# A table load and idle products ahead of the first transfers, and cross attention's probabilities scaled on VectorE

## The chip, the cores and the metric

The kernel runs on one core of a Trainium2 chip. The metric is device time in microseconds (us) of one execution; the median of the runs is compared. The engines are named as in the profile: PE is TensorE (PEld its weight loads), DVE is VectorE, ACT is ScalarE, POOL is GpSimd, SP is SyncE. A name with a q (ACTq, SPq) is the engine's queue of transfers.

## The reference

All data is float32, 256 tokens of width 1024. The first block mixes grouped attention and a gated spatial unit, adds cross attention over 256 memory tokens, and ends in a mixture of 16 experts. The second block (adaptive scaling, stick-breaking attention, retention, two more mixtures of experts) follows. What the change touches is the entry and this part:

```python
def memory_cross_attention(h, mem_n, w_cq, w_ckv, w_co):
    q = (h @ w_cq).reshape(B, S, X_HEADS, X_HEAD_DIM)          # 4 heads of 128
    kv = mem_n @ w_ckv
    ...
    s = jnp.einsum('bshd,bmhd->bhsm', q, k) * (X_HEAD_DIM ** -0.5)
    p = jax.nn.softmax(s, axis=-1)
    o = jnp.einsum('bhsm,bmhd->bshd', p, v).reshape(B, S, X_WIDTH)
    return o @ w_co
```

## The kernel before

Weights are streamed by SP in units of 1 MB (`Stream.load`, line 125) into a ring of buffers, in a plan written out ahead; a unit is asked for as soon as a buffer is free. A dense product in float32 is made of three products of rounded parts: every unit is split by ACT into a high part (`hl`, line 172, a cast) and by DVE into the rest (line 173), and the activations likewise (`h`, lines 510 and 511). PE then takes, for each quarter of a unit, high by high (line 424), high by rest (425) and rest by high (426). The expert stages use the weights as they are (line 1078).

A scheduler orders each engine's queue from the traced program by its own cost estimates; an instruction given to `keep_in_program_order` stays behind what was traced before it on its engine. The first splits and the `h` tiles are pinned in that way.

`setup` starts the transfers: `xT` on SP, the vectors `vec` on ACT's queue (line 460), the constants `cst`, `cs` and `tri` on POOL's. `block1` begins with the eight `h` tiles, scaled by columns of `vec`, among which the first unit is split in quarters. The first dense product (keys and values, 48 products of 256 columns) is emptied by `ev_kv`, and ahead of that `factors` (line 523) asks for the table that holds both logarithm and exponential (`lnexp`, line 273) and makes the root-mean-square factors of `x` from statistics on DVE (line 313). The next units' casts stand behind this on ACT.

In cross attention `xscores` makes the scores `xs` of a head on PE (line 726), and `softmax` takes the maximum on DVE (line 477), two exponentials with their sums on ACT (line 482), the reciprocal on DVE (line 484) and two scalings on ACT (line 487), each of 128x256. The four heads are traced one behind the other, with pieces of the values' product `cv` between. Then come, for every head, four transposes on PE (`cT`, line 496), a copy to SBUF on ACT (`cTT`, line 498), four products with the values (`co`, line 742), a cast (line 743) and a subtraction (line 744); and then the output's dense product, from line 424 again. `softmax` is also used by the first attention, with eight heads.

`warm(n)` (line 385) issues n products of 128x512 on a column of ones for nothing; the kernel before calls it in the routers and after attention. `lnexp` is an explicit load of a table; other table loads are placed by the compiler ahead of the first function that isn't in the table then loaded.

Of the kernel before, what the change touches and what calls it, by code (L numbers as in the profile page):

```python
# [25 lines left out]
AF = mybir.ActivationFunctionType  # L26
ALU = mybir.AluOpType
# [20 lines left out]
LOOK = [6, 14, 12, 5, 10, 12, 5, 12, 10, 15, 13, 16]  # L48


WARM_LOGITS, WARM_PLACES, WARM_INPUTS, WARM_AFTER = (4, 4, 4), (0, 4, 4), (4, 4, 4), (12, 12)


# [158 lines left out]
class Kernel:  # L212
# [238 lines left out]
    def setup(self):  # L451
        nc = self.nc
        self.C = self.keep("cst", [P, NCST])
        self.V = self.keep("vec", [P, NVEC])
        self.x = self.b8("x")
        self.tri = self.keep("tri", [P, P + 1], F32R)
        nc.gpsimd.memset(self.tri[:, P:].bitcast(F32), 1.0)
        self.ones = self.tri[:, P:]
        self.xT = self.b8("xT", F32, (P, 8, 256))
        nc.scalar.dma_start(self.V[:], self.ap["vec"])  # L460
        for k in (0, 4):
            nc.sync.dma_start(self.xT[:, k : k + 4].rearrange("p k t -> p (k t)"), self.ap["xT"][:, 256 * k : 256 * k + 1024])
        self.cs = self.b2("cs", F32, (P, 2, 2, 32))
        nc.gpsimd.dma_start(self.C[:], self.ap["cst"])
        nc.gpsimd.dma_start(self.cs[:].rearrange("p a t d -> p (a t d)"), self.ap["cs"])
        self.ident = self.cst(C_ID, P)
        tri = self.b2("tri", F32, (P, P))
        nc.gpsimd.dma_start(tri[:], self.ap["tri"])
        nc.gpsimd.tensor_copy(self.tri[:, :P], tri[:])


    def softmax(self, ps, scale, name):

        nc = self.nc
        s3 = ps[:].rearrange("p (a b) -> p a b", a=2)
        m = self.sm(name + "m", [P, 2])
        nc.vector.tensor_reduce(m[:], s3, AX, ALU.max)
        nc.vector.tensor_scalar(m[:], m[:], -scale, None, ALU.mult)
        e = self.b2(name + "e")
        s = self.sm(name + "s", [P, 2])  # L480
        for i in range(2):
            nc.scalar.activation(e[:, i * 256 : (i + 1) * 256], ps[:, i * 256 : (i + 1) * 256], AF.Exp, bias=m[:, i : i + 1], scale=scale, accum_out=s[:, i : i + 1])
        r = self.sm(name + "r", [P, 2])
        nc.vector.reciprocal(r[:], s[:])
        for i in range(2):
            q = e[:, i * 256 : (i + 1) * 256]
            nc.scalar.activation(q, q, AF.Copy, scale=r[:, i : i + 1])
        return e

    def probT(self, e, name):  # L490
# [11 lines left out]
    def block1(self):  # L502
        nc, tc = self.nc, self.tc
# [95 lines left out]
        for c2 in range(0, 5, 2):  # L599
            ps = self.aux("qT")  # L600
# [122 lines left out]
        def xscores(h):  # L723
            s = self.aux("xs")
            for qt in range(2):
                nc.tensor.matmul(s[:, qt * 256 : (qt + 1) * 256], cq[:, h, qt * P : (qt + 1) * P], ck[:, h, :], start=True, stop=True)
            return self.softmax(s, float(128 ** -0.5), "c")

        self.router(0)
        self.offsets(0)  # L730
        es = [xscores(h) for h in range(2)]
        for h in range(2, 4):
            next(fill)
            es.append(xscores(h))
# [1337 lines left out]
```

## Time and profile before

| | |
|---|---|
| runs, median (lowest to highest) | 1316.6 us (1316.1 to 1319.44), 3 runs |
| profiled execution, its own time | 1314.43 us |
| its span, first to last instruction | 1312.8 us |
| PE busy | 1241.5 us, 95% |
| DVE busy | 712.9 us, 54% |
| ACT busy | 405.0 us, 31% |
| POOL busy | 128.0 us, 10% |
| mean granted clock of TensorE | 0.984 |
| moved by DMA | 445.63 MB, mean 339 GB/s |

The profiled execution lies 2.2 us below the median of the runs. Busy shares are means over stages with different limits: PE's products are pipelined and their ends modelled, so 95% does not say that PE works at its peak.

### The profile page before, as it was taken

Reading aid. Unit: us, or ns where it says so; the run is one execution under the profiler, and the core shown is the slowest. Engines: PE = TensorE matmul, PEld = TensorE weight load, DVE = VectorE, ACT = ScalarE, POOL = GpSimd, SP = SyncE. Lnnn points to the kernel's source line nnn. Section 1 sums busy time; section 2 is a strip of 40 time slices with the busy share of each in tenths; the row PEclk is TensorE's granted clock in tenths of the full one; section 3 lists DMA queues with packets and bytes.
Section 4 is the critical chain, followed back from the end, with each engine's and each line's share of the span. In section 5 each row is a group of like instructions: output and inputs, shape, how many; then the busy total and the mean of one; then the engine's idle time right before and its main releaser. Section 6 shows DMA issues by size and latency. Waiting matters only on the chain. (4 is left out here: it accounts for less than half of the span.)

```text
span 1312.8 us, 18783 instructions
## 1 busy us (share of the span) xinstructions
PE 1241.5 (95%) x7149; PEld 784.2 (60%) x7149; DVE 712.9 (54%) x1422; ACT 405.0 (31%) x687; POOL 128.0 (10%) x136
## 2 busy tenths in 40 slices
PE   6999988899999989999999999989999999998995
PEld 5777867754334459977544334488988774433442
DVE  5898996433221149775742222378999754322224
ACT  5675534320100134653310001244345531100011
POOL 1000200000000020332001000130102100000101
PEclk9999998899999999999999999999999999999998
DMA  9857795769999998688499999997788577999992
GB/s 367 344 209 272 270 375 207 306 277 422 420 421 420 420 420 347 233 313 308 190 397 421 420 420 421 419 381 269 269 318 316 199 321 288 413 420 420 420 420 87
DMA packets 64497, 445.63 MB, mean 339 GB/s; under 512 B 7380, under 2 KB 7892, under 8 KB 12048
## 3 DMA queue, kind: packets, MB, share of 16 engines
q1 hardware_dynamic: 62352, 439.91, 83.9%
q10 hardware_dynamic: 1440, 3.13, 0.6%
q8 instruction: 59, 0.97, 0.3%
q0 software_dynamic: 608, 1.32, 0.3%
q14 instruction: 38, 0.31, 0.1%
HBM read 443.28 MB, written 1.05 MB: 338 GB/s over the span
## 5 line engine op out<-in xcount | busy, mean ns | idle before, releaser
L172 ACT CAST hl<-w 128x1024 fp32r<-128x1024 f32 (+1 forms) x160 | 164.7, 1039 | 174.2 <-PE dn L426 105.3
L173 DVE TENSOR_TENSOR hl<-w,hl 128x1024 fp32r<-128x1024 f32 (+1 forms) x154 | 191.4, 1252 | 49.5 <-ACT hl L172 49.3
L1078 PE MATMUL pg<-w,XT 128*64 128x512 f32 (+1 forms) x864 | 174.5, 601 | 0.0
L1078 PE MATMUL pu<-w,XT 128*64 128x512 f32 (+1 forms) x864 | 163.9, 597 | 0.0
L1078 PE MATMUL py<-w,hid 128*64 128x512 f32 (+2 forms) x912 | 155.7, 573 | 2.0 <-ACT hid L1093 2.0
L812 DVE SCALAR_TENSOR_TENSOR acc<-w,sc,acc 128x512 f32<-128x512 f32 x168 | 130.2, 779 | 1.6
L1090 DVE TENSOR_TENSOR hid<-hid,pu 128x512 f32<-128x512 f32 x21 | 14.4, 686 | 203.7 <-PE pu L1078 192.2
L1078 PEld LDWEIGHTS pu<-w,XT 128*64 128x64 f32 (+1 forms) x864 | 50.4, 126 | 96.8 <-issue 95.7
L1078 PEld LDWEIGHTS pg<-w,XT 128*64 128x64 f32 (+1 forms) x864 | 48.0, 125 | 93.2 <-issue 92.1
L1078 PEld LDWEIGHTS py<-w,hid 128*64 128x64 f32 (+1 forms) x912 | 48.8, 125 | 90.7 <-issue 81.8
L1131 DVE TENSOR_TENSOR x<-x,pc 128x512 f32<-128x512 f32 (+1 forms) x90 | 55.0, 647 | 32.8 <-PE pc L1129 32.2
L1066 PE MATMUL px<-O,xs 128*128 128x128 f32 x576 | 70.8, 276 | 0.0
L1399 ACT ACTIVATE hid<-pg 128x512 f32<-128x512 f32 x21 | 12.5, 597 | 187.2 <-PE pg L1078 187.2
L1066 PEld LDWEIGHTS px<-O,xs 128*128 128x128 f32 x576 | 67.2, 192 | 3.4 <-issue 3.4
L1117 DVE SCALAR_TENSOR_TENSOR y<-py,ws,gate 128x512 f32<-128x512 f32 x26 | 19.5, 751 | 66.0 <-PE py L1078 66.0
L1118 ACT CAST yh<-y 128x512 fp32r<-128x512 f32 x26 | 16.1, 618 | 120.8 <-DVE y L1117 120.8
L1070 POOL TENSOR_TENSOR XT<-XT,adaT 128x512 f32<-128x512 f32 x24 | 25.0, 1040 | 289.5 <-DVE XT L1068 289.5
L424 PE MATMUL dn<-hl,h 128*128 128x512 f32 (+1 forms) x128 | 49.4, 391 | 3.4 <-ACT hl L172 3.4
L424 PE MATMUL dn<-hl,e 128*128 128x512 f32 x128 | 51.2, 400 | 0.0
L425 PE MATMUL dn<-hl,h 128*128 128x512 f32 (+1 forms) x128 | 49.7, 388 | 0.8 <-DVE hl L173 0.8
L426 PE MATMUL dn<-hl,e 128*128 128x512 f32 x128 | 49.9, 390 | 0.0
L425 PE MATMUL dn<-hl,e 128*128 128x512 f32 x128 | 49.8, 389 | 0.0
(547 smaller groups left out, 2262.1 us busy)
## 6 DMA issues: line engine op xcount, KB each, us to landing
w<-e SPq DMA_DIRECT2D x282, 1024.0 KB, 14.2
w<-w SPq DMA_DIRECT2D x78, 1024.0 KB, 7.9
w<-wa SPq DMA_DIRECT2D x48, 1024.0 KB, 7.1
w<-e SPq DMA_DIRECT2D x12, 512.0 KB, 16.8
xT<-xT SPq DMA_DIRECT2D x2, 512.0 KB, 5.1
w<-w SPq DMA_DIRECT2D x4, 256.0 KB, 7.5
x<-x SPq DMA_DIRECT2D x2, 512.0 KB, 11.9
mem<-mem SPq DMA_DIRECT2D x2, 512.0 KB, 4.2
```

The lines of the kernel that those rows point to most:

```text
L172: a = k.nc.scalar.copy(hi, w)
L173: b = eng.tensor_sub(lo, w, hi.bitcast(F32))
L424: nc.tensor.matmul(o, a, wh[:, c, :], start=(first and c == 0), stop=False)
L425: nc.tensor.matmul(o, a, wl[:, c, :], start=False, stop=False)
L426: nc.tensor.matmul(o, b, wh[:, c, :], start=False, stop=(last and c == m - 1))
L812: pin(nc.vector.scalar_tensor_tensor(acc[:], w[:, j, :], c, acc[:], ALU.mult, ALU.add))
L1066: nc.tensor.matmul(ps[:, c * P : (c + 1) * P], xs[:, t * D + (k0 + c) * P : t * D + (k0 + c + 1) * P], O[:, t * P : (t + 1) * P].bitcast(F ...
L1070: nc.gpsimd.tensor_add(xo, xo, sh_v[:, k0 : k0 + 4].unsqueeze(2).to_broadcast([P, 4, P]))
L1078: nc.tensor.matmul(out[a : a + w, :], lhs[:, a : a + w], ws[e][(slice(None), c, *h)], start=start, stop=stop, tile_position=(0, a))
L1117: nc.vector.scalar_tensor_tensor(y, py, w, gate[:, n * 512 : n * 512 + 512], ALU.mult, ALU.mult)
L1118: nc.scalar.copy(yh, y)
L1131: nc.vector.tensor_add(a, a, pc)
```

## The change

`setup` asks for the table of logarithm and exponential and issues 20 idle products on the column of ones before its transfers. `softmax` gets a switch by which the two scalings run on DVE, and cross attention sets it; the first attention does not.

```diff
+WARM_START = 20
 WARM_LOGITS, WARM_PLACES, WARM_INPUTS, WARM_AFTER = (4, 4, 4), (0, 4, 4), (4, 4, 4), (12, 12)
...
         nc.gpsimd.memset(self.tri[:, P:].bitcast(F32), 1.0)
         self.ones = self.tri[:, P:]
+        self.lnexp()
+        self.warm(WARM_START)
         self.xT = self.b8("xT", F32, (P, 8, 256))
         nc.scalar.dma_start(self.V[:], self.ap["vec"])
...
-    def softmax(self, ps, scale, name):
+    def softmax(self, ps, scale, name, on_dve=False):
...
         for i in range(2):
             q = e[:, i * 256 : (i + 1) * 256]
-            nc.scalar.activation(q, q, AF.Copy, scale=r[:, i : i + 1])
+            if on_dve:
+                nc.vector.tensor_scalar(q, q, r[:, i : i + 1], None, ALU.mult)
+            else:
+                nc.scalar.activation(q, q, AF.Copy, scale=r[:, i : i + 1])
         return e
...
-            return self.softmax(s, float(128 ** -0.5), "c")
+            return self.softmax(s, float(128 ** -0.5), "c", True)
```

## Rows read from the trace of the kernel before

**Rows 1.** Windows: busy us of each engine, granted clock, DMA share, GB/s.

```profile
260.00:268.00 8.00, 8.00 (x61) 6.78 (x60) 7.05 (x50) 5.61 (x12) 0.00 (x0) 1.00 0.01 3
...
300.00:340.00 40.00, 40.00 (x256) 17.17 (x256) 7.19 (x17) 3.90 (x7) 0.00 (x0) 1.00 1.01 421
```

**Rows 2.** Timeline, 0 to 20 us: start, length, engine, line; idle before.

```profile
0.93 0.41 ACTq L460 DMA_DIRECT2D vec<-vec  x1
...
5.62 1.28 ACT L510 ACT_TABLE_LOAD   x1 [5.62 <-DMA xT<-xT]
...
6.91 0.91 ACT L510 ACTIVATE h<-xT,vec 128x256 fp32r<-128x256 f32 x2
...
9.35 0.62 ACT L172 CAST hl<-w 128x512 fp32r<-128x512 f32 x1 [1.53 <-DMA w<-w]
...
10.02 0.79 PE L424 MATMUL dn<-hl,h 128*128 128x256 f32 x2 [1.59 <-ACT hl L172]
...
14.49 2.00 ACT L172 CAST hl<-w 128x1024 fp32r<-128x1024 f32 x2 [0.57 <-DMA w<-w]
```

**Rows 3.** Windows of the first dense product.

```profile
10.00:14.00 4.00, 3.98 (x17) 3.75 (x18) 4.00 (x9) 3.92 (x9) 1.01 (x2) 1.00 1.02 422
14.00:18.00 4.00, 4.00 (x34) 4.00 (x34) 3.30 (x5) 3.29 (x3) 0.00 (x0) 1.00 1.04 410
```

**Rows 4.** Windows of two stretches ahead of and in cross attention.

```profile
196.00:200.00 4.00, 4.00 (x10) 3.10 (x10) 1.05 (x2) 0.00 (x0) 0.00 (x0) 0.50 0.03 12
...
232.00:236.00 4.00, 2.64 (x11) 2.04 (x11) 0.17 (x1) 2.80 (x9) 0.00 (x0) 0.57 1.01 424
```

**Rows 5.** Timeline of cross attention, 227 to 241 us.

```profile
227.19 1.02 PE L726 MATMUL xs<-ckv,cq 128*128 128x256 f32 x4
...
227.87 0.48 ACT L482 ACTIVATE ce<-xs,cm 128x256 f32<-128x256 f32 x1
...
229.01 0.67 DVE L477 TENSOR_REDUCE cm<-xs 128x2 f32<-128x512 f32 x1
229.13 0.91 ACT L487 ACTIVATE ce<-ce,cr 128x256 f32<-128x256 f32 x2 [0.23 <-DVE cr L484]
...
229.94 0.46 ACT L482 ACTIVATE ce<-xs,cm 128x256 f32<-128x256 f32 x1
...
232.94 0.58 ACT L498 COPY cTT<-cT 128x512 f32<-128x512 f32 x1
...
233.40 0.92 ACT L487 ACTIVATE ce<-ce,cr 128x256 f32<-128x256 f32 x2
...
234.25 1.06 PE L742 MATMUL co<-cTT,ckv 128*128 128x256 f32 x2
...
235.74 4.99 PE L742 MATMUL co<-cTT,ckv 128*128 128x256 f32 x14
...
240.38 0.58 PE L424 MATMUL dn<-hl,o 128*128 128x512 f32 x1
```

**Rows 6.** DMA issues: queue, count, KB each, median us to landing.

```profile
vec<-vec ACTq DMA_DIRECT2D x1, 115.5 KB, 4.8
...
tri<-tri POOLq DMA_DIRECT2D x1, 64.0 KB, 6.4
```

**Rows 7.** Timeline of ACT, 17 to 60 us.

```profile
20.98 0.20 ACT L283 ACTIVATE xn<-xnq 128x2 f32<-128x2 f32 x1 [3.19 <-DVE xnq L321]
...
23.02 3.88 ACT L172 CAST hl<-w 128x1024 fp32r<-128x1024 f32 x4
```

**Rows 8.** Timeline of PE, 20 to 32 us.

```profile
24.12 0.73 PE L424 MATMUL dn<-hl,h 128*128 128x512 f32 x2 [0.67 <-ACT hl L172]
26.01 0.50 PE L424 MATMUL dn<-hl,h 128*128 128x512 f32 x1 [1.15 <-ACT hl L172]
```

**Rows 9.** Groups of DVE by form: count, busy us, mean ns.

```profile
L1663 DVE TENSOR_SCALAR ang<-ang,cst 128x256 f32<-128x256 f32 x1 | 0.3, 350 | 0.0
```

**Rows 10.** Timeline of PE ahead of cross attention's scores.

```profile
195.96 0.79 PE L425 MATMUL cv<-hl,g 128*128 128x512 f32 x1 [3.61 <-DVE hl L173]
```

## The prediction

> **What bounds the kernel now.** I read the page's slices, then the stages by windows, then the two edited places in order of time. Between 300 and 340 us PE is busy for 40 of 40 us while the DMA engines are also full; just before that stage, at 260 to 268, DMA stands at 0.01 with PE full [rows 1]. The expert stages are thus fed by buffers that were filled long before, and they start when the serial work ahead of them is done: a microsecond gained or lost before 260 us moves everything behind it, one for one. Both edits lie before 260 us. So each is worth what it does to the end of its own stage, and I price those two stages alone.
>
> In the first stage the reader is to see who makes PE start at 10.02: the cast of the first weights, which itself waited 1.53 us for their transfer [rows 2]. The granted clock is written as 1.00 from the beginning, but the counts say otherwise: 17 products of 256 columns in 4 us, then 34 of them in the next 4 us, PE busy throughout [rows 3]. The first four microseconds therefore ran at 1.2 GHz and the next at 2.4.
>
> In cross attention ACT is the long queue and PE waits in short pieces. From 232 to 236 us the granted clock is 0.57 [rows 4], and the products of line 742 begin there: 14 of them take 4.99 us [rows 5].
>
> **The change, part by part. The table load.** It leaves 5.62, where it ran 1.28 us as soon as xT had landed, and goes to the head of ACT's queue [rows 2]. The `h` pair behind it can start up to 1.28 us sooner; but the next cast on ACT's queue waits for weights until 9.35 whatever is before it, after 1.53 us of idling [rows 2]. That idling only grows. Worth: 0.
>
> It now stands ahead of the `vec` transfer on the same queue, which went out at 0.93 [rows 2]. Bounds: not delayed at all, or issued at 0.93 + 1.28 = 2.21. Landing took 4.8 us for `vec` itself, 6.4 for the slowest small transfer [rows 6], so `vec` lands at 5.7 at best, 7.0 to 8.6 if delayed. The `h` pair takes 0.91 [rows 2], so it is done by 7.9 to 9.5, against the cast's 9.35. At worst 0.15 us late, and 0.57 us of waiting for the second unit's transfer at 14.49 stands behind as further cover [rows 2]. I take 0.
>
> The trace shows one length for the load, and the work behind it starts 0.01 us after it. The Trainium skill, ScalarE: Activation LUTs, section What ACT_TABLE_LOAD costs, counts a drain as well and arrives at about 2.66 us for a switch. By that figure, as an estimate, `vec` would be issued near 3.6 and land between 8.4 and 10.0, the pair would be done by 10.9, and after the cover some 1.0 us would be lost.
>
> The same table is still asked for by the later call in `factors`, as before; ACT idles 3.19 us just after it, waiting for DVE's statistics [rows 7]. Worth: 0.
>
> **The products for nothing.** They need only the memset, so they run from a little after 1 us. At 1.2 GHz 512 columns take 0.43 us, so 20 of them last 8.5 us at the very most and end by 9.7, before the first real product at 10.02 [rows 2]. With the clock rising after some 4 us, as it did there [rows 3], nine are slow and eleven take 0.235 each: they end near 7.7. Price on PE's path: 0.
>
> What they buy: 17 products at 4.0 / 34 = 0.118 us instead of 4.0 / 17 = 0.235 [rows 3], which is 2.0 us at most; less where a split is not ready. PE was through with all it had at 24.12 - 0.67 = 23.45 [rows 8], and would now be through at 21.45 or later. But the next product needs the cast that ACT starts at 23.02 [rows 7], and PE waited for that cast already, to 24.12, and for another of the same run to 26.01 [rows 8]. ACT got there late because of DVE's statistics of x (the 3.19 us), not because of PE. So the 2.0 us become idle time ahead of 24.12. I take 0; bounds: a gain of 2.0 if ACT's run came earlier too, and a loss (second rival).
>
> **The scaling.** Eight ACTIVATEs of line 487 leave ACT, in four pairs; a pair took 0.91 to 0.92 us [rows 5]. DVE gets eight tensor_scalars of 128x256. The nearest in the trace is the single one of line 1663, of this size, in SBUF, with one factor read from a tile: 350 ns [rows 9]. Consecutive ones overlap a little on this engine: I take 0.62 for a pair, between 0.70 (no overlap) and 0.55.
>
> The direct saving is on the last head alone: 0.92 - 0.62 = 0.3 us.
>
> Against it stands DVE's queue. There the maximum of head 2 (line 477, 0.67 us) begins at 229.01, after head 1's reciprocal [rows 5]. If head 1's pair of scalings goes in between, it begins about 0.55 later, and with it head 2's exponential. In before that exponential began at 229.94, at the instant ACT was through with head 1's scaling (229.13 + 0.91 = 230.04, of which 0.1 overlaps) [rows 5], so there is no slack to absorb it. The same again from head 2 to head 3: +1.1 us. The last head's scaled probabilities, complete at 233.40 + 0.92 = 234.32 in before [rows 5], come at 234.32 + 1.1 - 0.3 = 235.1.
>
> What pays for it is ACT. The copy of head 0's transposed probabilities waited for its turn on ACT until 232.94, and so head 0's product on PE until 234.25; from there 16 products of line 742 and the rest of the transposes stand in a row until 240.38, when line 424 starts [rows 5]. That tail is 240.38 - 234.32 = 6.1 us after the last scaling. With 3.7 us of scaling off ACT, two of the four copies (0.58 each) fit between the exponentials, and two heads' products move into PE's gaps. Eight products of 4.99 / 14 = 0.36 leave the tail: 2.9 us. Sum: 6.1 - 2.9 = 3.2 us of tail after 235.1 gives 238.3, a gain of 2.1. I take 2.0. Bounds: no product moves, 235.1 + 6.1 = 241.2, a loss of 0.8; three heads' products move, 4.3 us off the tail, a gain of 3.5.
>
> **Sum.** 0 + 0 - 2.0 on the profiled execution's own 1314.4 gives 1312.4. That execution stands 2.2 below the median of the runs, 1316.6, so the median should come to 1314.6.
>
> **Rivals.** First, DVE takes the maxima of heads 2 and 3 before the scalings, as they are ready: the last scores are done at 227.19 + 1.02 = 228.2 [rows 5]. Then the exponentials follow each other on ACT without the scalings, 229.94 - 227.87 - 0.91 = 1.16 us a head or less [rows 5], head 3's scaled probabilities are there near 227.87 + 3 x 1.16 + 0.8 = 232.1 instead of 234.3, and the tail is shortened as well or not: a gain of 2.2 to 5, I take 4: 1312.6. Against it: in before these maxima were put after the reciprocal although ready.
>
> Second, PE starves at the start. It would be idle from 21.45 to 24.12, and again up to 26.01, with 0.73 us of work in 4 us [rows 8]. Where PE was starved for 3.61 us at 195.96 [rows 10], the clock read 0.50 in the next 4 us [rows 4]. The Trainium skill (TensorE: Matmul & The Clock Gate, section Why this matters for your kernels) warns in the same sense against idle gaps between bursts; the row agrees. If the clock is lost here, 4 us at half speed after 26.01, the length of the slow start [rows 3], do 2 us of work: +2.0, which leaves 1314.6 + 2.0 = 1316.6.
>
> Third, and slower: DVE's queue delays heads 2 and 3, PE's order stays as it was (+0.8), and the longer gaps bring the low clock sooner or hold it longer, into the first 4 us of line 424: +2 more. 1316.6 + 2.8 = 1319.4. It decides as soon as head 0's product still stands behind head 3's transposes on PE.
>
> Fourth, nothing moves in PE's order and the clock behaves as before: +0.8, 1317.4. Fifth, that the products don't do what they say: if PE's idling from about 7.5 to 10.0 undoes the clock again, the start is as before, and the sum too. Sixth, `vec` lands later than any small transfer here, say at 9.5: the pair is done at 10.4, 1.05 late, 0.57 of it covered: +0.5, 1315.1.
>
> **How the numbers follow.** Forecast (with the fifth, and 0.05 for the sixth, which its own range takes in) 0.45, at 1314.6, itself 1313 to 1316; first rival 0.22; second 0.1; third 0.11; fourth 0.12. The range leaves out the farther part of the first and of the third: 1311.0 to 1319.2. A measurement of this kernel can tell about 0.3%, 3.9 us, from no change: below 1312.7 lie half of the first rival and a share of the forecast in which three heads' products move (0.2 in all); above 1320.5 only a third rival that is worse than priced (0.08); the rest, 0.72, is within.
>
> **What would show it.** Right: PE's early products spaced 0.12 at 11 us, line 424 still waiting for ACT near 24.1; in cross attention a product of line 742 ahead of head 3's transposes, and line 424 near 238. Wrong: `vec` landing after 8.6; a clock of 0.5 after 26; the maxima of line 477 beginning more than 0.6 us after the reciprocal, or before it; or an order of the queues far from the edits that has changed, since a scheduler sets it from its own estimates, and I have priced none of that.

## The result and the profile after

The changed kernel takes 1325.16 us (median of 7 runs, 1316.85 to 1327.24), the kernel before 1316.6 (7 runs, 1314.27 to 1319.44): a ratio of 1.0058, with an interval of 1.0043 to 1.0073. Ratios, here and below, are estimated from all the runs and are not quotients of the medians. The change costs 0.6% where a small gain was forecast, and the time lies above the range. Two later executions at a mean granted clock of 0.94 instead of 0.98, 1333.83 us of the kernel before and 1335.73 of the one with narrow products, belong to a slower state of the chip, and no reading rests on them.

The profiled execution is the quickest of the seven, at 1316.85 us; the other six took 1323.44 or more. So its profile shows what the edits did at their own places, and not where the usual loss is; for that the repeated run below is used. In both kernels the instructions stand in the same order on every engine, apart from the edited ones and one neighbour of theirs on DVE (line 818). Lines have new numbers: 172 is now 173, 424 is 425, 477 to 487 are 480 to 493 (the scaling on DVE is 491), 498 is 504, 742 is 748, 1078 is 1084, 1212 is 1218 and 1368 is 1374.

The start, in the timelines of ACT and of PE (start, length, engine, line; in brackets the idle time and what ended it):

```profile
0.93 1.28 ACT L274 ACT_TABLE_LOAD   x1 [0.93 <-PEq L2070]
0.96 0.40 ACTq L463 DMA_DIRECT2D vec<-vec  x1
5.74 0.91 ACT L516 ACTIVATE h<-xT,vec 128x256 fp32r<-128x256 f32 x2 [3.52 <-DMA vec<-vec]
9.23 0.62 ACT L173 CAST hl<-w 128x512 fp32r<-128x512 f32 x1 [2.59 <-DMA w<-w]
```

```profile
1.09 7.32 PE L386 MATMUL warm<-tri 128*128 128x512 f32 x20 [1.09 <-POOL tri L458]
...
9.90 0.51 PE L425 MATMUL dn<-hl,h 128*128 128x256 f32 x2 [1.28 <-ACT hl L173]
...
23.71 0.73 PE L425 MATMUL dn<-hl,h 128*128 128x512 f32 x2 [1.77 <-ACT hl L173]
25.60 0.51 PE L425 MATMUL dn<-hl,h 128*128 128x512 f32 x1 [1.16 <-ACT hl L173]
```

The load no longer stands between xT and the `h` pair, and `vec` went out at 0.96 while it ran. The idle time ahead of the cast grew from 1.53 to 2.59 us [rows 2]. The 20 idle products end at 1.09 + 7.32 = 8.41, and PE is idle for 1.28 us ahead of the first dense product. Against [rows 8] PE waits 1.77 us for the same cast instead of 0.67, so it was through at 21.94 instead of 23.45, and only 0.41 of these 1.5 us are left at 23.71.

The windows of the first dense product, of cross attention, and of the stretch where the usual loss will be seen:

```profile
10.00:14.00 4.00, 3.78 (x29) 3.56 (x30) 4.00 (x9) 3.96 (x10) 1.27 (x3) 1.00 1.02 421
...
232.00:236.00 4.00, 2.95 (x11) 2.29 (x12) 1.00 (x5) 1.98 (x6) 0.00 (x0) 0.50 1.01 426
236.00:240.00 4.00, 4.00 (x14) 3.31 (x13) 0.85 (x2) 2.18 (x5) 0.00 (x0) 0.66 1.00 416
```

29 products in the first four microseconds instead of 17 [rows 3]: in this execution the early clock was bought. It isn't in every one. The same window of the start alone, one of the experiments below:

```profile
10.00:14.00 4.00, 3.78 (x20) 3.69 (x20) 4.00 (x10) 3.48 (x8) 0.57 (x2) 0.60 1.01 418
```

Cross attention, in the timeline:

```profile
226.69 1.03 PE L732 MATMUL xs<-ckv,cq 128*128 128x256 f32 x4
...
227.37 0.48 ACT L485 ACTIVATE ce<-xs,cm 128x256 f32<-128x256 f32 x1
...
228.43 0.17 DVE L487 RECIPROCAL cr<-cs 128x2 f32<-128x2 f32 x1 [0.50 <-ACT ce L485]
228.51 0.67 DVE L480 TENSOR_REDUCE cm<-xs 128x2 f32<-128x512 f32 x1
229.09 0.60 DVE L491 TENSOR_SCALAR ce<-ce,cr 128x256 f32<-128x256 f32 x2
...
229.62 0.16 DVE L481 TENSOR_SCALAR cm<-cm 128x2 f32<-128x2 f32 x1
229.81 0.47 ACT L485 ACTIVATE ce<-xs,cm 128x256 f32<-128x256 f32 x1 [1.42 <-DVE cm L481]
...
233.22 1.07 ACT L504 COPY cTT<-cT 128x512 f32<-128x512 f32 x2
...
233.63 0.62 DVE L491 TENSOR_SCALAR ce<-ce,cr 128x256 f32<-128x256 f32 x2
...
234.37 1.06 PE L748 MATMUL co<-cTT,ckv 128*128 128x256 f32 x2
...
235.87 4.60 PE L748 MATMUL co<-cTT,ckv 128*128 128x256 f32 x14
...
240.11 0.58 PE L425 MATMUL dn<-hl,o 128*128 128x512 f32 x1
```

DVE takes a third order, which the prediction had not considered: reciprocal of head 1, maximum of head 2, the scalings of head 1, and only then the small multiplication (line 481) for which head 2's exponential waits. ACT idles 1.42 us there, and makes its copies in one piece after the last exponential. The fourth head's scores begin 0.50 us earlier than in [rows 5] and the dense product 0.27 earlier: this stage became 0.2 us longer. The 14 products in a row took 4.60 us here instead of 4.99, so at the same pace it would have been 0.6.

### The profile page after: what moved, and what is told of

It reads as the page before. It is cut to its first block, busy times and chain, and to the rows that moved or that the text cites. A ratio compares the mean times of both kernels' runs of the same rounds, so it can differ in the third digit from the quotient of the medians.

```text
span 1315.3 us, 18828 instructions
## 1 busy us (share of the span) xinstructions
PE 1248.4 (95%) x7169; PEld 789.7 (60%) x7169; DVE 715.1 (54%) x1430; ACT 401.8 (31%) x679; POOL 127.4 (10%) x136
```

## The experiments

Theories: the loss is at the start (PE's waits after the warm start bring the low clock early), in cross attention, or far from both. The kernels differ in their idle products, the place of the load and the scaling's engine.

**The change again.** No edit.

> The changed kernel itself, to see in a trace where its usual execution is longer. Theory A (the granted clock): the queues of both kernels hold the same instructions in the same order but for the edited ones, so no wait has been added; the extra time is stretches at the low clock in the expert stages, behind 250 us, and the trace shows more such windows than the kernel before, with about 8 us in sum. Theory B (a wait): the loss stands in one place, in cross attention or just behind it, with the clock as before. Time by both: 1323 to 1327.

Measured: 1325.11 us (1322.3 to 1326.71) against 1316.17, ratio 1.0064 (1.0051 to 1.0077). Its profiled execution took 1326.69 us and does hold the loss. Its PE timeline in the last expert stage:

```profile
1215.89 0.73 PE L1134 MATMUL pc<-yh,O 128*128 128x512 f32 x2 [1.07 <-ACTq L1374]
1216.62 0.72 PE L1135 MATMUL pc<-yl,O 128*128 128x512 f32 x2
1222.79 1.00 PE L1218 MATMUL pw<-cbr,O 128*128 128x32 f32 x4 [5.45 <-PEq L1374]
```

The same three lines before:

```profile
1210.93 0.73 PE L1128 MATMUL pc<-yh,O 128*128 128x512 f32 x2 [1.06 <-ACTq L1368]
1211.65 0.74 PE L1129 MATMUL pc<-yl,O 128*128 128x512 f32 x2
1212.94 0.62 PE L1212 MATMUL pw<-cbr,O 128*128 128x32 f32 x4 [0.55 <-DVE x L1131]
```

Between two neighbouring products PE waits 5.45 us instead of 0.55, for its own sequencer, at line 1374. That is the branch `with tc.If(more > 0)` which each expert stage has behind its rounds, for extra rounds. All instances of it on PE's sequencer (count; shortest, median and longest in ns; first and last start), in the repeated run, in the profiled execution of after, and before:

```profile
L1374 PEldq COMPARE_BRANCH  x3: 355/388/6004, 393.7 to 1216.6; - x3
```

```profile
L1374 PEldq COMPARE_BRANCH  x3: 358/468/473, 390.6 to 1211.4; - x3
```

```profile
L1368 PEldq COMPARE_BRANCH  x3: 358/367/482, 390.9 to 1211.7; - x3
```

In the repeated run the last of the three branches takes 6.0 us where the others take under 0.5. The profiled execution of after, the quick one, has no such branch.

The repeated run is also 2.8 us late by the end of cross attention. Its windows there and behind the branch:

```profile
24.00:28.00 4.00, 2.84 (x8) 1.96 (x9) 4.00 (x9) 2.77 (x3) 0.00 (x0) 0.80 1.01 422
28.00:32.00 4.00, 4.00 (x15) 3.19 (x15) 1.33 (x2) 0.00 (x0) 0.00 (x0) 0.78 1.01 422
...
1216.00:1222.00 6.00, 1.34 (x4) 0.48 (x4) 1.84 (x3) 0.00 (x0) 1.02 (x2) 0.63 1.02 416
1222.00:1228.00 6.00, 5.21 (x16) 2.21 (x18) 0.63 (x4) 0.00 (x0) 1.85 (x2) 0.51 1.01 416
```

So there are two candidates: the low clock after 26 us, which the second rival foresaw, and the branch with the low clock behind it. Neither theory fits alone: there is a wait, in the last expert stage and not in cross attention, and there are stretches at the low clock.

**The parts alone.** The start alone, the scaling alone, the idle products alone:

```diff
 # the start alone
-            return self.softmax(s, float(128 ** -0.5), "c", True)
+            return self.softmax(s, float(128 ** -0.5), "c")
 # the scaling alone
-        self.lnexp()
-        self.warm(WARM_START)
+        self.warm(0)
 # the idle products alone: no early lnexp(), and the scaling on ACT
-        self.lnexp()
         self.warm(WARM_START)
```

> The load and the 20 idle products at the start, the scaling on ACT as before. If the start costs the time: 1322 to 1327. If the scaling costs it: 1315.5 to 1317, some 0.4 us below the kernel before, which is what the first 60 us gained.

> The scaling on DVE alone, the start as before. If the scaling costs the time: 1322 to 1327. If the start does: 1316 to 1317.5, since line 425 behind cross attention starts within 0.3 us of where it did. If any shift of a fraction of a microsecond costs clock (theory A in its general form), this one and the start alone both come out off the kernel before, by several us.

> The 20 idle products alone, the table load where it was, the scaling on ACT. If the idle products cost the time, by what they do to the clock: 1322 to 1327. If the load or the scaling does: 1316 to 1317.

Measured against 1316.17: the start alone 1323.1, ratio 1.0048 (1.0034 to 1.0063); the scaling alone 1316.45, 1.0009 (0.9997 to 1.002); the products alone 1324.01, 1.0053 (1.0039 to 1.0067). The scaling changes nothing that the median or the ratio can tell, and the products by themselves carry the loss. With them the long branch is there: 6.22 us in the start alone, 6.24 in the products alone, 0.48 at most in the scaling alone.

**Narrow products.** Whether the loss comes from what the products do to PE's clock or from their being in the program: 20 of 16 columns instead of 512.

```diff
-    def warm(self, n):
+    def warm(self, n, cols=512):
...
-        self.lnexp()
-        self.warm(WARM_START)
+        self.warm(WARM_START, 16)
...
-            return self.softmax(s, float(128 ** -0.5), "c", True)
+            return self.softmax(s, float(128 ** -0.5), "c")
```

> 20 idle products of 16 columns instead of 512 ahead of the first transfers, load and scaling as in the kernel before: PE's program is longer by just as many instructions as in the change, but PE is idle again long before 5 us, so the start runs as before. If the place of the code behind it costs the time (theory C: the branch over the extra rounds of the last expert stage waits about 6 us for code): that branch takes 6 us again, and the time is 1321 to 1324. If it is the early clock alone (theory A): the branch takes 0.5 and the time is 1315.5 to 1317.5.

Measured: 1323.35 us against 1316.02, ratio 1.0058 (1.0035 to 1.0082). The profiled execution is the cleanest of all, since it keeps step with the one of before until the branch: the pair ahead of it begins at 1210.86, before at 1210.93. Its PE timeline and its branch:

```profile
1210.86 0.73 PE L1134 MATMUL pc<-yh,O 128*128 128x512 f32 x2 [1.07 <-ACTq L1374]
1211.59 0.73 PE L1135 MATMUL pc<-yl,O 128*128 128x512 f32 x2
1217.80 1.01 PE L1218 MATMUL pw<-cbr,O 128*128 128x32 f32 x4 [5.48 <-PEq L1374]
```

```profile
L1374 PEldq COMPARE_BRANCH  x3: 358/478/6045, 390.5 to 1211.6; - x3
```

And its windows from there, with one of the kernel before for the same work:

```profile
1217.80:1221.80 4.00, 4.00 (x12) 1.90 (x14) 0.63 (x4) 0.00 (x0) 1.85 (x2) 0.50 1.01 420
1222.20:1226.00 3.80, 3.80 (x22) 1.20 (x20) 0.00 (x0) 0.00 (x0) 0.00 (x0) 1.00 1.01 420
```

```profile
1212.90:1216.90 4.00, 3.96 (x20) 1.72 (x22) 1.21 (x5) 0.00 (x0) 0.27 (x1) 1.00 1.02 416
```

The wait is 5.48 - 0.55 = 4.9 us longer. Behind it the clock is at 0.50, and the first 4 us of work hold 12 products instead of 20: some 2 us more. The sum, 7, is close to the 1323.35 - 1316.02 = 7.3 between the medians. (The two profiled executions lie 8.6 apart. The other 1.7 is a second stretch of low clock, at 1258; the scaling alone has one there too, with a short branch.)

That the wait brings on the low clock right behind it is not shown. All four profiled executions with a long branch have it, but so have three of the ten with a short one: those with 8, with 14 and without products, described below. In the last of these PE waits only 0.55 us, and still:

```profile
1216.20 1.04 PE L1218 MATMUL pw<-cbr,O 128*128 128x32 f32 x4 [0.55 <-DVE x L1137]
1217.17 9.78 PE L1084 MATMUL pg<-w,XT 128*64 128x512 f32 x32
```

Before, the 32 products of the second line took 7.09 us.

**The count restored.** `warm` is also called behind the first two expert stages (ahead of the two attentions, not behind them as the expectations say); ten fewer there each give PE's program its old length by the time of the last stage. The load and the scaling are as in the kernel before. With 20 wide products at the start, with 20 narrow ones, and a third kernel, which fills the idle time between the second and the third unit with 8 idle products and takes 28 away later:

```diff
-WARM_LOGITS, WARM_PLACES, WARM_INPUTS, WARM_AFTER = (4, 4, 4), (0, 4, 4), (4, 4, 4), (12, 12)
+WARM_LOGITS, WARM_PLACES, WARM_INPUTS, WARM_AFTER = (4, 4, 4), (0, 4, 4), (4, 4, 4), (2, 2)
 # third kernel: 8 idle products ahead of the third unit, and
+WARM_LOGITS, WARM_PLACES, WARM_INPUTS, WARM_AFTER = (4, 4, 4), (0, 4, 4), (4, 4, 0), (0, 0)
```

> The 20 idle products of 512 columns at the start, and 20 fewer of the kernel's own idle products behind stick-breaking attention and retention (12 and 12 become 2 and 2), so that as many instructions stand ahead of the last expert stage's branch as in the kernel before. Theory C: the branch takes 0.5 again; what is left is the early loss of clock, 1317 to 1321. Theory A alone: 1322 to 1326, the branch plays no part.

> Both: 20 narrow idle products at the start and 20 fewer behind the two attentions, the control of the two others. Theory C: branch at 0.5, start as before: 1315.5 to 1318.5, the fewer products costing up to 2. Theory A: the same. The difference to the wide start with the same count is what the early clock alone costs: 1 to 4 us by both.

> The wide start, 8 more idle products between the second and the third unit, where PE starves, and 28 fewer of the kernel's own idle products before the last branch (again the count of before). If PE's starving between 21.5 and 23.7 loses the early clock: no low clock at 26, PE reaches the first attention's scores within 0.5 us of where the kernel before does unless the clock falls near 50, and the time is 1 to 3 below that of the wide start with the same count. If not, no difference.

Measured against 1316.02: 1318.44, ratio 1.0015 (1.0006 to 1.0024); 1317.89, 1.0011 (1.0003 to 1.002); 1318.48, 1.0016 (1.0007 to 1.0025). In the profiled executions of all three the branch is short again, here in the first:

```profile
L1374 PEldq COMPARE_BRANCH  x3: 355/362/388, 392.3 to 1213.2; - x3
```

Wide and narrow products differ by 0.55 us, less than the 1 to 4 expected, and the filling gives nothing: what they do to the early clock hardly reaches the end. (None of the three profiled executions has the low clock at 26, so they can't say whether filling would prevent it.) Some 2 us over the time of before remained to be explained.

**How many it takes.** 8 and 14 idle products instead of 20, none, and a control: the kernel before with the ten fewer behind each of the two stages.

```diff
 # the change, with fewer
-WARM_START = 20
+WARM_START = 8        # and 14; and self.warm(0)
 # the kernel before, for the control
-WARM_LOGITS, WARM_PLACES, WARM_INPUTS, WARM_AFTER = (4, 4, 4), (0, 4, 4), (4, 4, 4), (12, 12)
+WARM_LOGITS, WARM_PLACES, WARM_INPUTS, WARM_AFTER = (4, 4, 4), (0, 4, 4), (4, 4, 4), (2, 2)
```

> The change with 8 idle products at the start instead of 20. If what costs is where the branch's code lies, the price is a step: PE's branch in the last expert stage takes either about 6 us, and the kernel some 7 us more than before, or under 0.5 us, and the kernel within 2 us of before; nothing between. If every added product has its price (7 us by 20 products, 0.35 each), the kernel takes 2.8 us more, and the branch some 2.4.

> The change with 14 idle products. By the place of the code again one of two values, 6 us or under 0.5 us at the branch; if 8 products have the long branch, 14 should have it too, unless the next block begins between them. By a price for each product 4.9 us more than before.

> The kernel before with 2 idle products instead of 12 at the end of each of the first two expert stages, so with 20 products less in PE's program. It is the control of the run that has 20 at the start and 20 less there, which took 2 us more than before. If the 2 us come from the idle products that those two stages lost, this takes 2 us more than before (1318.5); if they come from the 20 products at the start, this takes what before takes (1316.3), and if 20 products less also move the branch out of its loaded code, 1323.

> The change with the early table load and the scaling on VectorE, but without the idle products. If the products alone carry the loss, 1316 to 1317, as before, with PE's branch under 0.5 us and a first transfer of vec no later than in the run with the products. If the load has a part in it, 1317.5 or more.

Measured against 1316.51: 8 products 1316.57, ratio 1.0007 (0.9996 to 1.0019); 14 products 1317.11, 1.0004 (0.9992 to 1.0016); none 1315.71, 0.9996 (0.9981 to 1.0012); the control 1317.28, 1.0002 (0.9992 to 1.0012). None of the four can be told from before, and none has the long branch in its profiled execution; here the one with 14:

```profile
L1374 PEldq COMPARE_BRANCH  x3: 355/362/388, 391.2 to 1210.6; - x3
```

For 0, 8 and 14 products no cost can be told, 20 cost 7 to 9 us: a step, not a price for each. More than 20 were not tried, so whether the branch stays long from there on is not known.

Single executions are less even than the medians. Of the 47 with the scaling on DVE and at most 14 products, 8 took 1320.2 to 1323.2 us; of the 90 of the kernel before, leaving out the one at 1333.83, none took over 1319.66. The one of the 8 that has a profile (no products, 1320.81) has a short branch, starts it 3.3 us later than before and loses another 3.1 behind it, to the low clock shown above. So the scaling may have a cost in some executions; what brings it about is open.

The control also answers the second rival: its start is that of the kernel before, without a product, and its profiled execution has the low clock of the repeated run at the same place:

```profile
24.00:28.00 4.00, 2.84 (x9) 1.92 (x9) 4.00 (x9) 2.54 (x3) 0.00 (x0) 0.82 1.02 424
28.00:32.00 4.00, 4.00 (x15) 3.19 (x14) 1.10 (x1) 0.00 (x0) 0.00 (x0) 0.75 1.01 418
```

So the low clock after 26 us also occurs without the change. The control is not slower by 2 us either, so the fewer products don't explain all of the 1.9 to 2.5 us that the three kernels with the count restored took more than before. That remainder stays open; its intervals overlap with the control's. No version beats the kernel before.

**What the branch waits for.** The page's list of DMA queues has one that carries instructions. Its row (packets, MB, share of the span) before and after:

```profile
q8 instruction: 59, 0.97, 0.3%
```

```profile
q8 instruction: 60, 0.98, 0.3%
```

It is 60 in the five profiled executions of kernels with 20 added products and nothing taken away, the quick one of after among them, and 58 or 59 in all the others. With the narrow products a packet runs in the microsecond from 1215 (the queue's row in that window), in the middle of the long branch, among DMA engines that are nearly full:

```profile
q1 hardware_dynamic: 55, 0.39, 94.6%
q8 instruction: 1, 0.02, 6.9%
```

Before, packets run at 1192 and again at 1215, behind the short branch; so a packet at 1215 alone proves nothing. But the count differs. From the start of the branch to 18.4 us later, with the narrow products and before:

```profile
q8 instruction: 3, 0.05, 1.1%
```

```profile
q8 instruction: 2, 0.03, 0.7%
```

It is three in all four executions with a long branch and two in all ten with a short one. In the quick execution of after, the additional one ran at 1209.1, 2.3 us ahead of the branch. This fits a branch whose target is in code not yet loaded: 40 more instructions on PE (a weight load and a product each) shift all that follows. The Trainium skill, Runtime: NRT & Kernel Launch, section Instruction fetch mechanics, states this mechanism: code comes in blocks of 256 instructions, in sequence, and a taken branch to a target outside the loaded blocks waits for a transfer. The step between 14 and 20 products and the one packet more agree with it. That section gives no length for the wait. The runs here show 6.0 to 6.2 us. Which engine a packet belongs to is not in the trace, so that the packet at 1215 is the target's is argued, not shown. Why it came ahead of the branch in one execution of thirteen (seven of the first comparison and six repeated) is open. So is the part of an instruction that PE has 46 to 50 us ahead of each of these branches, BRANCH_PREFETCH_HINT (the last one at 1165.7 with the narrow products and before alike): what it fetches the trace does not show, and no run leaves it out.

## Why the prediction was wrong

The step that failed is the price of the idle products, "Price on PE's path: 0". It counted the time in which they run, and there it was right: they end at 8.41, between the 7.7 forecast and the bound of 9.7, and ahead of the first dense product. It did not count that they are 20 weight loads and 20 products more in PE's program, ahead of a branch 1200 us later. That moved the branch into the case where it takes 6 us: 4.9 us of waiting, with some 2 lost to the low clock behind it in each of the profiled executions. That the added instructions do it is shown: 20 products with almost no work bring the long branch, and taking 20 others away ends it. That the wait is for code is argued. The text had named far-away effects as a thing not priced, but as a changed order of queues; the order did not change, and nothing in the prediction looked at branches. The view that would have raised the question was at hand: the branch's three instances with their lengths.

**Table load: 0.** Right. `vec` was not delayed by the load ahead of it, the lower of the two bounds. The estimate from the Trainium skill's page ScalarE: Activation LUTs, section What ACT_TABLE_LOAD costs, by which `vec` would go out near 3.6, does not agree: 0.96 was measured. The kernel with the load and without the products can't be told from before either.

**What the products buy: 0.** Right, with its mechanism, in the execution profiled: 1.5 us gained by 21.94 against at most 2.0, and 1.1 of it turned into more idle time ahead of 23.71. The fifth rival occurs as well: of six profiled executions with wide products, two have 20 and 23 products in the first 4 us instead of 29 to 31, at a clock of 0.60 and 0.71. By the prediction that changes nothing in the sum.

**Second rival, the clock lost at 26.** It did occur in the repeated run, but occurs in the control too, so the change isn't shown to cause it. It isn't needed for the loss either: the execution with narrow products has no such stretch and still ends 8.6 us later than before.

**Scaling: -2.0.** Wrong in size and in its main term. The pair on DVE takes 0.60 to 0.62 us, as priced. The last scaled probabilities are there at 233.63 + 0.62 = 234.25, against 234.32 in a stage that now begins 0.5 earlier, so 0.4 late (0.8 was priced). But no product moved: the first two of line 748 still begin behind head 3's first transpose and 14 stand in a row, and the tail is 240.11 - 234.25 = 5.9 us instead of 6.1, not 3.2. The term of 2.9 us for the shortened tail is what failed; it took for granted that a freed ACT would make its copies between the exponentials. It made them after them. That is the fourth rival's order on PE, at 0.2 us instead of 0.8 (0.6 at the pace of before), and alone it can't be told from no change.

## What to carry to other kernels

Added instructions are not free because an engine is idle: they push all later code of that engine, and a branch far behind them can become long. Here 14 products cost nothing that could be told, and 20 cost 7 to 9 us. When a change loses far from its edit and the order of the queues is the same, compare the lengths of the branch instructions; the same number of instructions with almost no work in them shows whether the place or the work costs. And one profiled execution may be the odd one: here the only one of seven without the loss was the one on the page.

## What the runs showed of the hardware

A branch on PE's sequencer took 355 to 482 ns in its usual case and 6.0 to 6.2 us in the other, and in those four executions the clock was at 0.50 to 0.51 for the first 4 us of work behind it; with a short branch it was at 0.50 to 0.58 there in three of ten. A transfer issued by ACT went out at 0.96 while the table load ahead of it on the same engine ran from 0.93 to 2.21. The stretches of low clock are at different places in executions whose programs have the same start: from 24 to 32 us the clock read 1.00 in the kernel before and 0.82 and 0.75 in its control; from 52 to 56 it read 1.00 with the narrow products and 0.50 in the kernel with the same start and 20 products fewer later.
